# A two-layer hybrid attention block with the order of every engine worked out by the framework's other timing model

## The chip, the cores and the metric

The kernel runs on one core of one Trainium2 chip. The metric is the time of one execution on the device in microseconds (us). Before the change it is 3184.43 us, the median of 3 runs (3184.01 to 3186.54). A core has four compute engines that the profile names PE (TensorE, matrix products), ACT (ScalarE), DVE (VectorE) and POOL (GpSimd), and SP (SyncE), which issues the transfers here; PEld is the loading of TensorE's weights, which overlaps its products. Each engine works through its own list of instructions in order.

## The reference, cut to what matters

Two layers over 256 context and 1024 latent tokens of width 1024, in fp32. In each layer one wide projection feeds four branches, each of width 256; their outputs are projected, gated, summed and projected out.

```
p = (layer_norm(x) * (1 + scale) + shift) @ w_in           # and the same for the context tokens
A: neighbourhood attention, 4 heads of 64 (window 8x16 with a bias, plus all context)
B: latent attention, 4 heads of 96 (64 + 32 rotary)         softmax(q k^T * scale) v, keys: context + latent
C: bidirectional RG-LRU (conv of width 4, one linear scan per direction)
D: grouped-query attention, 4 query heads of 64 over 2 key heads
acc = sum_i sigmoid(m_i) * ((y_i * silu(z_i)) @ w_branch_i)
x   = layer_norm(alpha * x + gate * (acc @ w_out)) * ln_g + ln_b
```

## The kernel before

Every fp32 product is made of three: each operand is split into a high and a low part, and high x high, high x low and low x high are summed (`mm_a`, L271 to L273, and `mm_b`, L279 to L281). Normalized, modulated tokens stand in SBUF, transposed, as `xh` and `xl` for a whole layer.

A layer goes through these stages, which the names in the trace begin with: `g_proj` (projections of D), then `m_proj` and `a_proj` (projections of B and A) woven with `lru` (C) and `g_att` (attention of D), then `m_att` (attention of B), `a_att` (attention of A), `merge`, `last` (the fourth branch's merge) and `outp`. The names `start` and `outp` also stand for the DRAM buffers that were made in those stages. A name of the trace carries no number of the layer; by time, what lies before 1745 us is layer 0.

Attention reads its operands from DRAM. For each head of A and B, and each pair of heads of D, `load_k` (L641) fetches the keys, high rows over low rows, as a tile `ks` of 128 x 1280 (640 KB), and `load_v` (L646) the values, `vs`. A head is worked in units of two query tiles. `load_q` (L632, and L634 for the rotary rows of B) fetches the queries of a unit into one of two `q` buffers; the scores (L618, for A's windows L839) go to PSUM, DVE copies them into a score tile `p` (`pa` in A) with their maxima, and the softmax runs in place on ACT (exp at L592) and DVE. `values` transposes the score tile by blocks of 128 keys (L552), ACT and DVE split the result into two parts (L284, L285), and L568 and L569 multiply it by the values. `values` of a unit is put off until the scores of a later one have been emitted (`defer`), so that scores and values of neighbouring units alternate. Meanwhile `tick` doles out steps of `gates()`, products for the merge that serve as filling for TensorE (L279 to L281 in `m_att` and `a_att`).

The tiles `ks`, `vs`, `p`, `pa`, `y`, and A's bias tables `be` and `bm` share one pool of 12 slots:

```
sl = ctx.enter_context(tc.tile_pool(name="sl", bufs=12))
def load_k(d, blk, r0):
    t = slot(F32R, s="ks")
    sp.dma_start(t.bitcast(F32), d[:, blk, r0:r0 + 64, :])
```

A tile takes a slot when one comes free; its first writer waits for the last reader of the tile that held the slot.

The order of the work is not the order of the Python program. The program emits all instructions once; the framework's `TileContext` then simulates them with a model of the time of each, and from this it decides the order on every engine, which slot each tile gets, and so what each waits for. No order is written by hand.

Of the kernel before, what the change touches and what calls it, by code (L numbers as in the profile page):

```python
# [45 lines left out]
def hybrid_kernel(ctx: ExitStack, tc, a):  # L46
    nc = tc.nc
# [26 lines left out]
    def weave(*streams):  # L74
        """run step generators side by side, in proportion to their expected numbers of steps"""
        live = [[0, n, label, gen] for label, gen, n in streams]
        while live:
            s = min(live, key=lambda s: (s[0] + 0.5) / s[1])
            phase[0] = s[2]
            s[0] += 1  # L80
            if next(s[3], live) is live:
                live.remove(s)
# [3 lines left out]
    def tick(w=1.0):  # L86
        """emit the share of the filling steps that goes with w units of work"""
        fill["due"] += w * fill["rate"]
        while fill["due"] >= 1.0:
            fill["due"] -= 1.0  # L90
            if next(fill["gen"], fill) is fill:
                fill["rate"] = fill["due"] = 0.0
# [20 lines left out]
    def spare():  # L113
        """a [128, 512] tile out of all that are free outside of the branches"""
        turns[0] += 1
        tag = ("tmp", "ph", "tmp", "pl", "tmp", "ph", "pl")[turns[0] % 7]
        return tp.tile([128, 512], F32, tag=tag, name=nm("spare"), bufs=3 if tag == "tmp" else 2)
# [33 lines left out]
    def modulation(l, base, ncols, out, stage, sw):  # L151
        """out["m"] [128, 2, n]: column chunks of silu(cond) @ w_mod + b_mod for both conditions"""
        acc = ps_v.tile([128, 512], F32, tag="pv", name=nm("pm"))
        g = 4
        w_ = ncols // g
        n = ncols // 128
        bm = lc.tile([128, 16], F32, tag="bm", name=nm("bm"))
        sp.dma_start(bm[:, :n], a["b_mod"][l, :, base // 128:base // 128 + n])
        for k in range(KC):
            for h in range(ncols // sw):  # L160
                w = stage()
                c0 = base + h * sw
                sp.dma_start(w, a["w_mod"][l, k * 128:(k + 1) * 128, c0:c0 + sw])
                for j in range(sw // w_):
                    q = 32 * (h * sw // w_ + j)
                    pe.matmul(acc[q:q + 2, :w_], sc[:, k, :], w[:, j * w_:(j + 1) * w_],
                              start=k == 0, stop=k == KC - 1)
                yield
        tps = tbank()
        for j in range(g):  # L170
            row = tmp()
            act.copy(row[0:2, :w_], acc[32 * j:32 * j + 2, :w_])
            for i in range(w_ // 128):
                c = j * (w_ // 128) + i
                pe.transpose(tps[:, 2 * c:2 * c + 2], row[0:2, i * 128:(i + 1) * 128], ident[0:2, 0:2])
        mc = lc.tile([128, 2, 16], F32, tag="modc", name=nm("modc"), bufs=4)
        dve.tensor_tensor(mc[:, :, :n].rearrange("p s n -> p n s"),
                          tps[:, :2 * n].rearrange("p (n s) -> p n s", s=2),
                          bm[:, :n, None].to_broadcast([128, n, 2]), ALU.add)
        if n == 16:  # L180
            dve.tensor_scalar(mc[:, :, 8:16], mc[:, :, 8:16], 1.0, None, ALU.add)
        out["m"] = mc
        yield
# [82 lines left out]
    def mm_a(ps, xs, ws, n0, n1, first=True, last=True):  # L266
        """ps[tok, n] = sum_k x[:, k]^T w[k][:, n0:n1] with operands in two exact parts."""
        nk = len(ws)
        for k in range(nk):
            (xh, xl), (wh, wl) = xs(k), ws[k]  # L270
            pe.matmul(ps, xh, wh[:, n0:n1], start=first and k == 0, stop=False)  # L271
            pe.matmul(ps, xh, wl[:, n0:n1], start=False, stop=False)
            pe.matmul(ps, xl, wh[:, n0:n1], start=False, stop=last and k == nk - 1)  # L273
# [13 lines left out]
    def layer(l, xh, xl, need_ctx, gate, finish, side, side2, ahead=None):  # L287
# [27 lines left out]
        def put_t(dst, t, first, src, rows=128):  # L315
            """transpose column blocks of src [tok, 128*n] to dst[first+i][:, tile t] in two parts"""
            n = len(src)
# [13 lines left out]
        def put_v(dst, t, src3):  # L331
            """src3 [tok, heads, 64] -> per head (high | low) parts"""
            n = src3.shape[1]
            vt = tp.tile([128, 4, 128], F32R, tag="ph", name=nm("vt"), bufs=2)
            hi_lo(vt[:, :n, :64], vt[:, :n, 64:], src3)
            sp.dma_start(dst[t * 128:(t + 1) * 128], vt.bitcast(F32)[:, :n, :])

        def rope(y, t2, h, e, cs, sn, t):
            """axial rotation of y [tok, h, 4*e] in place; t2 [tok, h*4*e] is scratch"""
            w = 4 * e  # L340
# [9 lines left out]
        def project(ws, first_col, n, take=mm):  # L350
            """tokens @ weights tile by tile; the last two together, which frees the weights sooner"""
            for t in range(TT - 2):
# [11 lines left out]

# [1 line left out]
        def g_steps():  # L366
# [43 lines left out]

# [1 line left out]
        def put_u(i, c, y):  # L412
            """branch output times silu of its gate, to DRAM"""
            w = load_chunk(w_in, C_Z + 256 * i + 128 * c)
# [10 lines left out]
        def lru_steps():  # L425
            cols = lc.tile([128, 22], F32, tag="lrucols", name=nm("lrucols"), bufs=1)
            sp.dma_start(cols, a["lru_cols"][l])
            cw, cb, ba, bx, lam = cols[:, 0:8], cols[:, 8:10], cols[:, 10:14], cols[:, 14:18], cols[:, 18:22]
            # -8 * softplus(-lam), softplus by max(-lam, 0) + 2 atanh(e / (2 + e)), e = exp(-|lam|)
            f = [lc.tile([128, 4], F32, tag=f"sp{i}", name=nm("sp"), bufs=1) for i in range(5)]  # L430
# [19 lines left out]
            for c in range(2):  # L450
# [30 lines left out]
                for d in range(2):  # L481
# [16 lines left out]
                    act.activation(r, r, AF.Exp, scale=ca[:, dc])  # L498
                    # 1 - a^2 = t (1 + a^2), t = tanh(-log a)
                    h = slot(s="lruo")  # L500
# [18 lines left out]

# [1 line left out]
        later = []  # L521

        def defer(f, keep):
            """run f after the stages put off before it, all but the newest keep of them now"""
            later.append(f)
# [3 lines left out]
        def attend(h, y, units, loadq, scores, vt):  # L529
            """units: (query tiles, value blocks); rows of y that belong to head h get the output"""  # L530
            o = 64 * (h % 2)
# [52 lines left out]
        def softmax(pt, mx, ns, spans, scale, qi):  # L584
            """rows of pt hold scores / scale with segment maxima mx; spans: column ranges in use"""
            nb = small(1, "nb")
# [40 lines left out]
        def load_q(d, blk, r0, t0, nq, rope=None):  # L627
            """moving side of the scores: the high rows twice, the low rows twice, and the rope rows"""
            t = tp.tile([128, 3, 256], F32R, tag="q", name=nm("q"), bufs=2)
# [8 lines left out]
        def load_k(d, blk, r0):  # L638
            """high rows over low rows"""
            t = slot(F32R, s="ks")  # L640
# [7 lines left out]

# [1 line left out]
        def g_att():  # L650
# [10 lines left out]

# [1 line left out]
        pre = []  # L663

        def m_load():
            """tables and raw weights of the latent branch, ahead of their use"""
            tab = slot(w=896, s="mtab")
# [93 lines left out]

# [1 line left out]
        def m_att():  # L763
# [15 lines left out]

# [1 line left out]
        def a_steps():  # L781
# [15 lines left out]

# [1 line left out]
        def a_att():  # L799
# [72 lines left out]
        def gates():  # L872
            """the merge gates, before their sigmoid, of the branch that is merged last, to DRAM"""
            for c in range(KC):
# [23 lines left out]

# [1 line left out]
        acc = [None] * KC  # L900
# [38 lines left out]

        # the last branch: its gates are there; the sum goes in two parts where xm was  # L940
        phase[0] = f"last{l}"
# [31 lines left out]

# [1 line left out]
        phase[0] = f"outp{l}"  # L975
# [48 lines left out]
    def xm_group(t0, nt):  # L1024
        """xm of nt tiles, one block of channels at a time"""
        s = 1 if t0 < CT else 0
# [64 lines left out]
def _constants(np):  # L1091
    """arrays that depend on the shapes alone"""
    pos = np.arange(SEQ)
# [74 lines left out]
```

## Time and profile before

| | |
|---|---|
| median of the runs | 3184.43 us |
| span of the profiled execution | 3176.4 us |
| TensorE busy | 2806.6 us (88%) |
| loading of TensorE's weights | 2317.9 us (73%) |
| VectorE busy | 1659.0 us (52%) |
| ScalarE busy | 1382.4 us (44%) |
| GpSimd busy | 208.7 us (7%) |
| transfers, mean | 88 GB/s |
| chain that ended last | PE 63%, DMA 17%, DVE 5%, ACT 4%, SP's queue 3% |

The profile gives one execution on the chip. Its own time is that span; the medians of the runs count 8.0 us more, which lie around the span. Busy shares are means over stages of different kinds, so the table says little about any one of them: the merge keeps TensorE nearly always busy, the attention stages do not. In a row of the view of busy time by stretch, further down, stand the start and end, the length, the busy time of PE, PEld, DVE, ACT and POOL with their numbers of instructions, the granted TensorE clock as a share of full speed, the busy share of the 16 DMA engines, and GB/s. The stages of layer 0 in the trace: `g_att` with projections about 300 to 548 us, `m_att` 548 to 832, `a_att` 832 to 1091, `merge` 1091 to 1570; of layer 1, in the same order: 1994 to 2213, 2213 to 2476, 2476 to 2708, and 2708 to 3035.

### The profile page before, as it was taken

What the parts mean: (1) busy time and instruction counts of PE and PEld (TensorE: products, weight loads), DVE (VectorE), ACT (ScalarE), POOL (GpSimd) and SP (SyncE); (2) the same over time, 40 slices, a digit from 0 to 9 for tenths busy, and PEclk for the clock granted to TensorE, in tenths of its full rate; (3) what the DMA queues carried; (4) which work ended last, traced back from release to release, by engine and by line L of the source; (5) the groups of instructions that cost most, each with busy time, mean ns of one, the idle gap of its engine ahead of it and who ended that gap; (6) DMA issues with size and microseconds to landing.
All of it is one profiled execution on the core that took longest, in us unless ns stands there. A gap on an engine that the chain in (4) does not pass through costs nothing.

```text
span 3176.4 us, 40938 instructions
## 1 busy us (share of the span) xinstructions
PE 2806.6 (88%) x14798; PEld 2317.9 (73%) x14798; DVE 1659.0 (52%) x4049; ACT 1382.4 (44%) x2546; POOL 208.7 (7%) x273
## 2 busy tenths in 40 slices
PE   7999978778878999999999899878777688999998
PEld 4787767666767877777768787667666576888877
DVE  5666655555555512232377656556566456223356
ACT  4366655545555512121234456555555455222230
POOL 1200000000000000000042210000000100000031
PEclk9999989888988999999999999999898889999999
DMA  7233222211233322222353323222212222222142
GB/s 264 80 105 117 63 77 80 77 61 64 65 101 95 92 68 65 63 77 62 99 185 101 117 76 116 84 70 74 77 56 72 86 76 90 77 60 60 54 149 84
DMA packets 304563, 281.01 MB, mean 88 GB/s; under 512 B 23400, under 2 KB 249960, under 8 KB 304360
## 3 DMA queue, kind: packets, MB, share of 16 engines
q1 hardware_dynamic: 304360, 278.40, 28.4%
q8 instruction: 116, 1.90, 0.2%
q14 instruction: 87, 0.71, 0.1%
HBM read 207.67 MB, written 70.66 MB: 88 GB/s over the span
## 4 chain that ended last, share of the span: by engine, by line
PE 63%; DMA 17%; DVE 5%; ACT 4%; SPq 3%; issue 2%; POOL 2%; DVEq 0%; POOLq 0%; ACTq 0%
PE merge__mm L279 6%; PE merge__mm L280 6%; PE merge__mm L281 6%; PE m_att__s L618 3%; DMA m_att__q<-start__qkm 2%; PE a_att__mm L279 2%; PE a_att__mm L280 2%; PE a_att__mm L281 2%; DMA m_att__ks<-outp__qkm 2%; SPq L632 2%; PE m_att__t L552 2%; PE a_att__t L552 2%; PE merge__s L279 2%; PE merge__s L280 2%; PE merge__s L281 2%
## 5 line engine op out<-in xcount | busy, mean ns | idle before, releaser
L279 PE MATMUL merge__mm<-xh,merge__whi 128*128 128x512 f32 (+1 forms) x960 | 360.3, 375 | 0.0
L281 PE MATMUL merge__mm<-xh,merge__wlo 128*128 128x512 f32 (+1 forms) x960 | 354.8, 370 | 0.0
L280 PE MATMUL merge__mm<-xl,merge__whi 128*128 128x512 f32 (+1 forms) x960 | 354.8, 370 | 0.0
L279 PEld LDWEIGHTS merge__mm<-xh,merge__whi 128*128 128x128 f32 x960 | 181.5, 189 | 63.1 <-issue 21.6
L618 PE MATMUL m_att__s<-m_att__ks,m_att__q 128*128 128x512 f32 (+1 forms) x400 | 126.7, 387 | 96.9 <-DMA m_att__ks<-outp__qkm 47.4
L233 ACT CAST merge__whi<-merge__wraw 128x512 fp32r<-128x512 f32 x144 | 79.1, 551 | 290.4 <-PE merge__mm L280 243.9
L281 PEld LDWEIGHTS merge__mm<-xh,merge__wlo 128*128 128x128 f32 x960 | 181.6, 189 | 30.7
L280 PEld LDWEIGHTS merge__mm<-xl,merge__whi 128*128 128x128 f32 x960 | 181.7, 189 | 28.9
L928 ACT ACTIVATE merge__tmp<-merge__mm 128x512 f32<-128x512 f32 (+1 forms) x120 | 66.4, 553 | 312.0 <-PE merge__mm L281 311.2
L234 DVE TENSOR_TENSOR merge__wlo<-merge__wraw,merge__whi 128x512 fp32r<-128x512 f32 x144 | 86.4, 601 | 193.3 <-ACT merge__whi L233 187.9
L620 DVE TENSOR_SCALAR_CACHE_REDUCE m_att__p<-m_att__s 128x512 f32<-128x512 f32 (+1 forms) x200 | 113.7, 588 | 115.3 <-PE m_att__s L618 114.3
L284 ACT CAST m_att__ph<-m_att__t 128x512 fp32r<-128x512 f32 x164 | 94.5, 584 | 171.7 <-PE m_att__t L552 126.3
L934 DVE TENSOR_TENSOR merge__tmp<-merge__s,merge__tmp 128x512 f32<-128x512 f32 (+1 forms) x80 | 51.1, 638 | 220.6 <-PE merge__s L281 220.6
L618 PEld LDWEIGHTS m_att__s<-m_att__ks,m_att__q 128*128 128x128 f32 x400 | 76.3, 206 | 112.3 <-DMA m_att__ks<-outp__qkm 42.2
L285 DVE TENSOR_TENSOR g_att__pl<-g_att__t,g_att__ph 128x512 fp32r<-128x512 f32 x154 | 104.7, 688 | 84.8 <-ACT g_att__ph L284 70.9
L618 PE MATMUL g_att__s<-g_att__ks,g_att__q 128*128 128x512 f32 (+1 forms) x400 | 110.0, 381 | 38.6 <-DMA g_att__ks<-outp__qkg 19.6
L285 DVE TENSOR_TENSOR m_att__pl<-m_att__t,m_att__ph 128x512 fp32r<-128x512 f32 x164 | 111.1, 687 | 55.6 <-ACT m_att__ph L284 54.9
L620 DVE TENSOR_SCALAR_CACHE_REDUCE g_att__p<-g_att__s 128x512 f32<-128x512 f32 (+1 forms) x200 | 112.0, 586 | 42.2 <-PE g_att__s L618 41.3
L284 ACT CAST g_att__ph<-g_att__t 128x512 fp32r<-128x512 f32 x154 | 88.1, 583 | 100.6 <-PE g_att__t L552 52.4
L568 PE MATMUL g_att__pv<-g_att__ph,g_att__vs 128*128 128x256 f32 x308 | 98.1, 326 | 30.6 <-ACT g_att__ph L284 29.9
L279 PE MATMUL a_att__mm<-xh,a_att__whi 128*128 128x512 f32 (+1 forms) x304 | 119.0, 391 | 1.6 <-ACT a_att__tmp L885 1.6
L962 POOL TENSOR_TENSOR merge__acc<-merge__acc,last__spare 128x512 f32<-128x512 f32 (+1 forms) x40 | 55.9, 1421 | 939.0 <-DVE last__spare L961 938.8
(425 smaller groups left out, 7870.4 us busy)
## 6 DMA issues: line engine op xcount, KB each, us to landing
merge__wraw<-in_w_in_dram SPq DMA_DIRECT2D x96, 256.0 KB
mod__wm<-in_w_mod_dram SPq DMA_DIRECT2D x48, 256.0 KB
g_proj__wm<-in_w_mod_dram SPq DMA_DIRECT2D x16, 512.0 KB
a_att__wraw<-in_w_in_dram SPq DMA_DIRECT2D x32, 256.0 KB
last__wraw<-in_w_out_dram SPq DMA_DIRECT2D x32, 256.0 KB
merge__wraw<-in_w_branch_dram SPq DMA_DIRECT2D x48, 128.0 KB
g_att__q<-start__qkg SPq DMA_DIRECT2D x40, 128.0 KB
m_att__q<-start__qkm SPq DMA_DIRECT2D x40, 128.0 KB
```

The costliest lines, as they stand in the source:

```text
L233: act.copy(hi[:, :n], raw[:, :n])
L234: dve.tensor_sub(lo[:, :n], raw[:, :n], hi[:, :n])
L279: pe.matmul(ps, wh, xh, start=first and k == 0, stop=False)
L280: pe.matmul(ps, wh, xl, start=False, stop=False)
L281: pe.matmul(ps, wl, xh, start=False, stop=last and k == nk - 1)
L284: act.copy(hi, src)
L285: dve.tensor_sub(lo, src, hi)
L552: pe.transpose(tb[:n, c:c + 128], pts[qi][:, col:col + n], ident)
L568: pe.matmul(pv[:, :nq], vt[:n, vb, :], ph[:n, w], start=first, stop=False)
L618: pe.matmul(s[:, :w], qs[:, j, qi * 128:(qi + 1) * 128], k[:, c0:c0 + w], start=j == 0, stop=j == len(ks) - 1)
L620: dve.tensor_scalar(pt[:, c0:c0 + w], s[:, :w], scale, None, ALU.mult, ALU.max, accum_out=mx[:, ns:ns + 1])
L928: act.activation(sgm[:, :g[1]], pm[:, :g[1]], AF.Sigmoid)
```

## The change

One argument is passed to the framework, and comments and docstrings are blanked, which leaves every line number as it was:

```
-    with tile.TileContext(nc) as tc:
+    with tile.TileContext(nc, schedule_with_timeline_sim=True) as tc:
```

With it the framework simulates the same emitted instructions with another timing model, and takes the order on each engine and the slots of the pools from that. The two programs hold the same 14670 matrix products and the same 1260 transfers of SP; ACT's table loads, which the framework puts in after the order is fixed, go from 77 to 54 (at L420, the sigmoid of the branches' gates, from 27 to 15; at L592, the exp, from 22 to 12; L957 from 2 to none; L433 from 1 to 2). In the merge stages few products move; in the attention stages nearly all do.

The first place is TensorE in `m_att` of layer 1, where the scores of the second head (its K tile is `ks_4740`) have ended and those of the third (`ks_4880`) are about to begin. Before, the rows ahead of the first score of the new head are transpositions of the tiles `p_4812` and `p_4820`, the second last unit of the old head, products with the values, and filling:

```order
L569 MATMUL m_att1__pv_4828_21492<-m_att1__pl_4843_21547,m_att1__vs_4741_21180 128x256
L568 MATMUL m_att1__pv_4828_21492<-m_att1__ph_4842_21546,m_att1__vs_4741_21180 128x256
L569 MATMUL m_att1__pv_4828_21492<-m_att1__pl_4843_21547,m_att1__vs_4741_21180 128x256
L552 MATMUL m_att1__t_4866_21630<-ident_90,m_att1__p_4812_21444 128x128
L552 MATMUL m_att1__t_4866_21630<-ident_90,m_att1__p_4820_21468 128x128
L552 MATMUL m_att1__t_4866_21630<-ident_90,m_att1__p_4812_21444 128x128
L552 MATMUL m_att1__t_4866_21630<-ident_90,m_att1__p_4820_21468 128x128
L279 MATMUL m_att1__mm_4775_21293<-xh_102,m_att1__whi_4623_20698 128x512
L280 MATMUL m_att1__mm_4775_21293<-xl_103,m_att1__whi_4623_20698 128x512
L281 MATMUL m_att1__mm_4775_21293<-xh_102,m_att1__wlo_4624_20699 128x512
L618 MATMUL m_att1__s_4886_21710<-m_att1__ks_4880_21698,m_att1__q_4883_21703 128x512
```

After, what stands ahead of it belongs to the head's first unit (`p_4743`, `p_4751`), without filling:

```order
L568 MATMUL m_att1__pv_4794_21364<-m_att1__ph_4799_21379,m_att1__vs_4741_21180 128x256
L569 MATMUL m_att1__pv_4794_21364<-m_att1__pl_4800_21380,m_att1__vs_4741_21180 128x256
L568 MATMUL m_att1__pv_4794_21364<-m_att1__ph_4799_21379,m_att1__vs_4741_21180 128x256
L569 MATMUL m_att1__pv_4794_21364<-m_att1__pl_4800_21380,m_att1__vs_4741_21180 128x256
L552 MATMUL m_att1__t_4804_21400<-ident_90,m_att1__p_4743_21187 128x128
L552 MATMUL m_att1__t_4804_21400<-ident_90,m_att1__p_4751_21211 128x128
L552 MATMUL m_att1__t_4804_21400<-ident_90,m_att1__p_4743_21187 128x128
L552 MATMUL m_att1__t_4804_21400<-ident_90,m_att1__p_4751_21211 128x128
L568 MATMUL m_att1__pv_4794_21364<-m_att1__ph_4802_21392,m_att1__vs_4741_21180 128x256
L618 MATMUL m_att1__s_4886_21710<-m_att1__ks_4880_21698,m_att1__q_4883_21703 128x512 x2
L618 MATMUL m_att1__s_4886_21710<-m_att1__krs_4582_20569,m_att1__q_4883_21703 128x512
```

Between the last score of the old head and the first of the new one there are now 8 transpositions and 9 products of 256 columns, where there were 8 transpositions, 4 such products and 6 of filling; the transpositions lag the scores by more units than before.

The second place is SP at the same head. `[waits ...]` names the engines and DMA queues on which an entry waits. Before, the K load stands behind the queries of the head's first unit, and the V load right behind it:

```order
L632 DMA m_att1__q_4883_21703<-outp0__qkm_3479_15831 128x1x256 [waits DMAHW2_49,DMAHW1_49,DMAHW7_49,DMAHW0_49,PE_49]
L634 DMA m_att1__q_4883_21703<-outp0__qkm_3479_15831 64x1x256
L632 DMA m_att1__q_4883_21703<-outp0__qkm_3479_15831 128x1x256
L634 DMA m_att1__q_4883_21703<-outp0__qkm_3479_15831 64x1x256
L641 DMA m_att1__ks_4880_21698<-outp0__qkm_3479_15831 128x1x1280 [waits DMAHW3_49,DVE_49]
L646 DMA m_att1__vs_4881_21700<-outp0__vm_3482_15834 128x10x128 [waits DMAHW4_49,Activation_49]
L632 DMA m_att1__q_4934_21915<-outp0__qkm_3479_15831 128x1x256 [waits DMAHW6_49,DMAHW5_49,PE_49]
```

After:

```order
L632 DMA m_att1__q_4883_21703<-outp0__qkm_3479_15831 128x1x256 [waits DMAHW2_49,DMAHW1_49,DMAHW3_49,DMAHW0_49,PE_49]
L634 DMA m_att1__q_4883_21703<-outp0__qkm_3479_15831 64x1x256
L632 DMA m_att1__q_4883_21703<-outp0__qkm_3479_15831 128x1x256
L634 DMA m_att1__q_4883_21703<-outp0__qkm_3479_15831 64x1x256
L641 DMA m_att1__ks_4880_21698<-outp0__qkm_3479_15831 128x1x1280 [waits DMAHW4_49,PE_49]
L632 DMA m_att1__q_4934_21915<-outp0__qkm_3479_15831 128x1x256 [waits DMAHW6_49,DMAHW7_49,DMAHW5_49,PE_49]
L634 DMA m_att1__q_4934_21915<-outp0__qkm_3479_15831 64x1x256
L632 DMA m_att1__q_4934_21915<-outp0__qkm_3479_15831 128x1x256
L634 DMA m_att1__q_4934_21915<-outp0__qkm_3479_15831 64x1x256 [waits DMAHW0_49]
L646 DMA m_att1__vs_4881_21700<-outp0__vm_3482_15834 128x10x128 [waits DMAHW1_49,DVE_49,PE_49]
```

The V load went behind the queries of the second unit, and the K load now waits for PE: its slot is that of `ks_4740`, the K tile of the head before, and is freed by that head's last score. Before, its slot was that of `p_4743`, freed by a transposition well ahead of that.

## Rows read from the trace of the kernel before

**Rows 1.** Busy time by stretch: attention stages of both layers, and layer 0's merge.

```profile
300.00:548.00 248.00, 211.73 (x1332) 185.26 (x1331) 154.93 (x446) 148.19 (x244) 0.00 (x0) 0.93 0.24 75
548.00:832.00 284.00, 215.29 (x1246) 186.73 (x1245) 153.45 (x433) 146.31 (x236) 0.00 (x0) 0.87 0.23 72
832.00:1091.00 259.00, 224.88 (x1321) 195.17 (x1322) 140.69 (x464) 139.75 (x292) 20.28 (x24) 0.91 0.27 84
1091.00:1570.00 479.00, 471.67 (x2317) 364.35 (x2316) 123.78 (x214) 89.56 (x172) 0.00 (x0) 0.99 0.26 71
...
1994.00:2213.00 219.00, 181.76 (x1141) 157.88 (x1141) 137.62 (x387) 126.40 (x198) 0.00 (x0) 0.94 0.23 72
2213.00:2476.00 263.00, 196.88 (x1143) 169.92 (x1143) 144.62 (x391) 136.47 (x207) 0.00 (x0) 0.88 0.23 72
2476.00:2708.50 232.50, 192.76 (x1064) 160.63 (x1065) 121.93 (x413) 125.94 (x256) 20.02 (x24) 0.90 0.27 85
```

**Rows 2.** What PE waited for: total us, times, longest.

```profile
PE m_att__s L618 <- DMA m_att__ks<-outp__qkm: 47.4, 4, 14.4
PE a_att__s L839 <- DMA a_att__q<-outp__qka: 37.2, 6, 14.6
PE m_att__s L618 <- DMA m_att__ks<-start__qkm: 33.3, 3, 12.1
PE g_att__pv L568 <- ACT g_att__ph L284: 29.9, 10, 8.2
PE a_att__s L618 <- DMA a_att__q<-start__qka: 19.7, 4, 10.2
PE g_att__s L618 <- DMA g_att__ks<-outp__qkg: 19.6, 2, 12.0
PE m_att__pv L568 <- ACT m_att__ph L284: 15.5, 3, 6.9
PE m_att__s L618 <- DMA m_att__q<-start__qkm: 14.7, 10, 2.9
...
PE a_att__s L839 <- DMA a_att__ks<-outp__qka: 11.0, 1, 11.0
PE g_att__s L618 <- DMA g_att__ks<-start__qkg: 10.6, 1, 10.6
PE a_att__s L618 <- issue: 9.3, 1, 9.3
```

**Rows 3.** PE in order of time: start, length, what, idle before it and its releaser.

```profile
412.93 1.19 PE L618 MATMUL g_att__s<-g_att__ks,g_att__q 128*128 128x256 f32 x4 [10.57 <-DMA g_att__ks<-start__qkg]
...
680.14 0.28 PE L569 MATMUL m_att__pv<-m_att__pl,m_att__vs 128*128 128x256 f32 x1
680.26 0.60 PE L552 MATMUL m_att__t<-ident,m_att__p 128*128 128x128 f32 x4
680.62 0.36 PE L568 MATMUL m_att__pv<-m_att__ph,m_att__vs 128*128 128x256 f32 x1
...
686.48 0.28 PE L281 MATMUL m_att__mm<-xh,m_att__wlo 128*128 128x256 f32 x1
697.51 0.77 PE L618 MATMUL m_att__s<-m_att__ks,m_att__q 128*128 128x256 f32 x2 [10.75 <-DMA m_att__ks<-start__qkm]
...
2583.39 0.77 PE L839 MATMUL a_att__s<-a_att__ks,a_att__q 128*128 128x512 f32 x1 [4.66 <-DMA a_att__q<-outp__qka]
```

**Rows 4.** SP's DMA issues around one new head, in order of time.

```profile
677.50 1.43 SPq L641 DMA_DIRECT2D m_att__ks<-start__qkm  x1
678.97 2.79 SPq L646 DMA_DIRECT2D m_att__vs<-start__vm  x1
684.17 10.31 SPq L632 DMA_DIRECT2D m_att__q<-start__qkm  x1
```

**Rows 5.** Busy time while only that head's K load was left.

```profile
686.00:696.00 10.00, 0.76 (x5) 0.49 (x3) 0.91 (x2) 3.67 (x6) 0.00 (x0) 0.79 0.13 52
```

**Rows 6.** ACT's table loads at the sigmoid: busy, mean ns.

```profile
L420 ACT ACT_TABLE_LOAD x27 | 34.6, 1283 | 5.7 <-DVE lru__lruo L422 5.2
```

## The prediction

> **What bounds the kernel now.** The profiled span is 3176.4 us; the median of the runs, 3184.43, is 8.0 above it. The view of busy time by stretch comes first. In the merge TensorE is busy 471.7 of 479 us at a granted clock of 0.99: nothing is to be had there but fewer products, and the order of a merge hardly moves. In the six attention stretches the difference of length and busy time is 36.3, 68.7, 34.1, 37.2, 66.1 and 39.7 us, together 282, and the granted clock is 0.87 to 0.94 [rows 1]. The change must win or lose there. No other engine is the bound: VectorE, the next, is busy 121 to 155 us in each of them.
>
> The view of what TensorE waited for says on what. Eight of the rows are first scores of a new head (L618, L839) that wait for its K tile or its queries: 47.4 + 37.2 + 33.3 + 19.7 + 19.6 + 11.0 + 10.6 + 9.3 = 188 us. Two more are products with the values that wait for the split of the transposed scores (L568 behind L284): 29.9 + 15.5 = 45.4. Queries inside a head cost little: 14.7 us in 10 waits, the longest 2.9 [rows 2].
>
> The timeline shows how a head's start stalls. In the third head of layer 0's latent attention SP issues the K load at 677.50, the V load at 678.97, and the next unit's queries at 684.17 [rows 4]; TensorE has work until 686.48 + 0.28 and then stands 10.75 us, till the K tile is there at 697.51 [rows 3]. So 20.0 us go by from issue to use, of which 9 are covered. From 686 to 696 little but this load is in flight, and it moves 52 GB/s on 0.13 of the 16 engines, that is on 2 of them [rows 5]. At that rate its 640 KB need 12.6 us. A head therefore starts without a stall only if 12.6 to 20 us of TensorE's work lie between the moment when the K load can go out and its first use.
>
> **The change part by part.**
>
> *K loads of ten heads.* The order shown at the third head of layer 1's latent attention is the pattern: the K load now needs the slot that the K tile of the head before leaves with its last score. From there to the first use stand 8 transpositions, 9 products of 256 columns and a half-filled score. In the trace a product of 256 columns goes by in 0.12 us and four transpositions in 0.36 (680.14 to 680.26, 680.26 to 680.62) [rows 3]; so 2 x 0.36 + 10 x 0.12 = 1.9 us of work remain to cover the load. I counted all twenty heads in this way. In ten the slot is now freed late, with these covers: second head of D 8.0 us in layer 0 and 1.1 in layer 1; first head of B 3.3 and 4.5; third of B 2.4 and 1.9; first of A 2.4 and 1.9; third of A 5.7 and 1.7. They sum to 32.9 us; by the same count the ten slots were free 12 to 32 us ahead of the use. In the trace these ten heads stalled 77.5 us: eight stalls from 10.57 (at 412.93) to 4.66 (at 2583.39), and two heads without one [rows 3].
>
> A K load takes 12.6 us by its rate or 20.0 by the whole way from issue to use. The way shown had a V load of the same size right behind it, which the new order sends later, so I go between them, nearer to the lower: 16. Then the ten heads stall 10 x 16 - 32.9 = 127 us (93 to 167), which is **+50 us** (+16 to +90).
>
> *Other head starts.* In layer 1's attention A the queries of a head went out behind K, V and both bias loads; now they go right behind K. Two stalls of that kind, at the second and fourth heads, lie in the row of 37.2 us [rows 2]; they can lose as much as V and bias held them up: **-15** (-26 to 0). The first head of D in layer 0 loses cover, 13 us to 6 to 10: **+8** (0 to +10).
>
> *Second units.* In layer 0 the second unit of a head now comes 0.7 to 3.5 us of TensorE's work after the first (2.5 to 14 before), and its queries stand right behind the K load on SP. Such an entry took 10.31 us to go out behind K and V [rows 4]. For eight such heads I take 2 us each, about what query waits cost now [rows 2]: **+15** (0 to +50, where 6 of the 10.31 show each time). Elsewhere the time from a free query buffer to its use falls from some 12.5 us of work to 8: **+5** (0 to +15).
>
> *Transpositions and values.* The new order puts more TensorE work between a transposition and its product with the values, 2.6 to 4.5 us at the median against 1.7, so waits behind the split should shrink. But the longest of them, 8.2 and 6.9 us [rows 2], are not of that kind: they are ACT standing behind something late, which 3 us don't cover. And the steps of filling, which lay between, now come in blocks. I take **-15** of the 45.4 (-45 to +30).
>
> *Table loads.* 23 fewer, at 1283 ns [rows 6], are 29.5 us of ACT. ACT is busy about 126 to 148 us of stretches of 219 to 284 [rows 1], so most of it lies beside other work: **-5** (-29.5 to 0). The Trainium skill (ScalarE: Activation LUTs, What ACT_TABLE_LOAD costs) adds a drain of some 1380 ns to each switch; the row shows the 1283, and none shows the drain. By the page 23 loads would give ACT 61 us back; were all of it on the path, the sum would be 43 + 5 - 61 = -13, an estimate that speaks against a slower kernel and falls into the first rival below.
>
> *Merge, projections, output:* nearly the same order, **0** (-5 to +5).
>
> Sum: 50 - 15 + 8 + 15 + 5 - 15 - 5 = +43 us. Span 3176.4 + 43 = 3219; with the 8.0 around it **3227 us**, 1.3% slower.
>
> **The rivals.**
>
> *It gets faster by what the new order does better.* A head's slot was free early before, and yet most heads stalled: the load's way, not the slot, may be what counts. If K loads without V and bias behind them land in the 12.6 us of their rate, the ten heads cost +16 at most. Then the queries of A give back 26, values 45, and table loads some 10; second units cost 10. That is 16 - 26 - 45 - 10 + 10 = -55: about 3130. For it speaks that the waits of L568 start at ACT [rows 2], which has 23 loads less; against it, that 1 to 8 us of cover are less than the 12.6 us of the rate alone, so that no row lets a head start without a stall.
>
> *Nothing much moves.* Stalls change places: the ten heads +16 to +30, the queries and values -30. Time 3180 to 3190. For it: before, too, eight of the ten stalled, and a stall can grow only by the cover lost. Against it: this asks several terms of different causes to cancel.
>
> *Much slower.* The queries are late as well. Each second unit then waits behind the K load on the same queue (+50), the ten heads stand the full 20 us (+90), and filling in blocks leaves the values' waits as they are (0). With the falling clock behind longer stalls (0.87 where they are thickest, 0.99 without them [rows 1]) that is 140 - 15 + 8 + 5 - 5 = +133: about 3317. For it: a query entry took 10.31 us to go out behind K and V. Against it: V goes later now.
>
> *The argument does nothing that TensorE feels:* excluded by the order, in which nearly all attention products move.
>
> **How the numbers follow.** Forecast +43, its own range +10 to +90: 45%. Much slower, beyond +90: 18%. Little moves, -10 to +10: 13%, half of it inside what counts as no change (0.2%, 6.4 us, about what a measurement of this kernel can tell). Faster beyond -10: 24%. So faster 0.27, the same 0.08, slower 0.65. The range leaves out about a tenth on either side: 3135 to 3300.
>
> **What would show it.** Right: in the profile after, first scores of a new head wait for `ks` in at least seven of the ten heads, 11 to 18 us each, and the sum of the head rows goes from 188 to 220 or more; the second and fourth head of A in layer 1 stall less; SP issues the K load within 2 us of the old head's last score. Wrong: if the K tiles land within 13 us of their issue and the head rows sum to less than 190; if waits of L568 fall by more than 30 us or grow beyond 70; or if the merge stretches, which I hold at zero, move by more than 10 us.

## The result, and the profile after

The changed kernel takes 3450.36 us (median of 4 runs, 3447.23 to 3453.35), the kernel before 3185.48 beside it: a ratio of 1.082, 95% interval 1.0801 to 1.0838. It is 265 us slower. The forecast was slower by 1.3%, 3227 us, with 3300 as the upper end; the direction was right and the size far off.

The spans of the two profiled executions, on which all readings below rest, lie 275 us apart and not 265. In every run with both figures a time is only 1.7 to 2.2 us above its span, so most of the 8.0 us that the prediction adds to the span before is that this execution was a faster one than the median.

The page of the profile after: its span, TensorE's busy time, and TensorE's granted clock in 40 slices in tenths.

```profile
span 3451.5 us, 41058 instructions
...
PE 2877.8 (83%) x14798; PEld 2384.5 (69%) x14798; DVE 1669.8 (48%) x4049; ACT 1352.0 (39%) x2523; POOL 206.4 (6%) x273
...
PEclk9998988978799899999999999879978879999999
```

The span grew by 275.1 us. TensorE is busy 71.2 us longer with the same products, and so idle 203.9 us longer. The view of busy time by stretch says where; its columns are those of [rows 1], the stretches are those between the first scores of successive attention stages, layer 0's merge (1253 to 1721), and layer 1's projections up to its first attention score (1902 to 2180).

```profile
337.00:592.00 255.00, 202.72 (x1164) 175.62 (x1164) 152.75 (x454) 130.93 (x216) 0.00 (x0) 0.89 0.22 69
592.00:933.00 341.00, 248.39 (x1394) 214.52 (x1395) 161.59 (x448) 146.69 (x242) 0.00 (x0) 0.84 0.20 64
933.00:1253.00 320.00, 247.38 (x1369) 211.35 (x1369) 141.97 (x470) 140.16 (x298) 19.54 (x24) 0.87 0.23 71
1253.00:1721.00 468.00, 465.60 (x2304) 362.34 (x2304) 123.04 (x212) 89.03 (x173) 0.00 (x0) 1.00 0.27 71
...
1902.00:2180.00 278.00, 236.28 (x1173) 201.63 (x1171) 158.71 (x334) 136.50 (x307) 34.83 (x58) 0.92 0.31 95
2180.00:2421.00 241.00, 173.11 (x1012) 148.39 (x1012) 132.02 (x374) 116.58 (x181) 0.00 (x0) 0.87 0.20 64
2421.00:2712.00 291.00, 212.82 (x1234) 184.53 (x1234) 148.94 (x400) 136.48 (x211) 0.00 (x0) 0.87 0.21 66
2712.00:2987.00 275.00, 205.35 (x1103) 172.20 (x1103) 127.01 (x421) 123.94 (x259) 19.55 (x24) 0.86 0.24 73
```

All six attention stretches lost: 255 us against 248, 341 against 284 and 320 against 259 in layer 0, 241 against 219, 291 against 263 and 275 against 232.5 in layer 1. Their granted clock was 0.87 to 0.94 before [rows 1] and is 0.84 to 0.89. The merge did not lose: its stretch is 468 us at 1.00, where it was 479 at 0.99, and TensorE is busy 6 us less in it, with 13 products fewer. Ahead of the attention both layers lost. Layer 0 reaches its first attention score at 337 us and not at 301, and layer 1 reaches its own 278 us after its projections begin, where it took 249 at a granted clock of 0.96:

```profile
1745.00:1994.00 249.00, 225.75 (x1153) 190.02 (x1151) 158.76 (x334) 137.87 (x302) 38.11 (x56) 0.96 0.34 104
```

What TensorE waited for, the view of [rows 2] after the change (total us, times, longest):

```profile
PE m_att__s L618 <- issue: 47.3, 3, 18.3
PE a_att__s L839 <- DMA a_att__q<-start__qka: 46.4, 14, 12.1
PE a_att__s L839 <- DMA a_att__q<-outp__qka: 37.9, 10, 12.5
PE m_att__s L618 <- DMA m_att__ks<-start__qkm: 36.1, 3, 12.9
PE m_att__s L618 <- DMA m_att__ks<-outp__qkm: 34.7, 2, 22.4
PE g_att__s L618 <- DMA g_att__ks<-outp__qkg: 32.7, 2, 18.4
...
PE m_att__s L618 <- DMA m_att__q<-start__qkm: 26.7, 17, 3.5
...
PE g_att__pv L569 <- DVE g_att__pl L285: 17.6, 30, 4.6
PE g_att__s L618 <- DMA g_att__q<-start__qkg: 15.1, 11, 2.5
...
PE g_att__pv L568 <- ACT g_att__ph L284: 11.2, 12, 2.1
PE a_att__mm L279 <- ACT a_att__tmp L885: 11.0, 10, 2.0
```

Two such rows before, which [rows 2] leave out:

```profile
PE g_att__pv L569 <- DVE g_att__pl L285: 4.3, 5, 2.5
...
PE a_att__s L839 <- DMA a_att__q<-start__qka: 3.0, 2, 2.3
```

Most of the large rows are still first scores of a head; the three waits of the first row, for which the profile shows no releaser (issue), are such too. New are the many small ones: at L839 A's queries in layer 1 make TensorE wait 10 times instead of 6 [rows 2], in layer 0 14 times instead of 2, and `g_att__pv L569` waits 30 times for DVE's low part of the transposed scores, where it waited 5 times. The longest wait of L568 in D's attention, 8.2 us before [rows 2], is 2.1.

Two sums over all of TensorE's records put this in order. By the length of the idle piece, before and after: 0.3 to 3 us, 93 pieces with 99 us and 210 with 228; 3 to 6 us, 39 and 44 us; over 6 us, 21 pieces in both, 214 and 281 us. So 129 of the 204 us are short waits, and 67 are long ones. By what the product behind it was: first scores of a head 178 to 249 us, first scores of a unit with new queries 0 to 44, other scores 45 to 82, products with the values 63 to 53, transpositions and filling 2 to 30, everything outside of the attention 71 to 107. (The 9 us that are left in either profile lie at the ends of the span. The prediction's 188 us for first scores are 10 more than the 178, because the rows for A's queries hold waits inside heads too.)

The busy time follows from the clock: TensorE ran at 1.2 GHz, the lower of its two levels, for 344 us before and for 597 after, and 191 and 323 us of its busy time fall in there. Products of 256 columns follow each other 0.21 us apart at that level (2552.95 to 2553.16 in the trace after) and 0.12 at the full one [rows 3]. If about half of the busy time at the lower level is loss, it is 95 and 162 us: 66 more, an estimate, and nearly all of the 71.

### The profile page after: what moved, and what is told of

Read it like the earlier page. It is cut to its first block, busy times and chain, and to the rows that moved or that the text cites. A ratio compares the mean times of both kernels' runs of the same rounds, so it can differ in the third digit from the quotient of the medians.

```text
span 3451.5 us, 41058 instructions
## 1 busy us (share of the span) xinstructions
PE 2877.8 (83%) x14798; PEld 2384.5 (69%) x14798; DVE 1669.8 (48%) x4049; ACT 1352.0 (39%) x2523; POOL 206.4 (6%) x273
## 4 chain that ended last, share of the span: by engine, by line
PE 60%; DMA 19%; DVE 7%; ACT 7%; issue 4%; SPq 3%; POOL 0%; POOLq 0%; DVEq 0%; ACTq 0%
PE merge__mm L279 6%; PE merge__mm L280 6%; PE merge__mm L281 6%; DMA a_att__q<-start__qka 3%; PE m_att__s L618 2%; DMA m_att__q<-start__qkm 2%; PE a_att__mm L279 2%; PE a_att__mm L280 2%; PE a_att__mm L281 2%; PE merge__s L280 1%; PE merge__s L281 1%; PE merge__s L279 1%; PE m_att__t L552 1%; PE g_att__s L618 1%; PE a_proj__mm L271 1%
## 5 line engine op out<-in xcount | busy, mean ns | idle before, releaser
L285 DVE TENSOR_TENSOR m_att__pl<-m_att__t,m_att__ph 128x512 fp32r<-128x512 f32 x164 | 111.5, 687 | 72.2 <-ACT m_att__ph L284 71.2
L618 PEld LDWEIGHTS g_att__s<-g_att__ks,g_att__q 128*128 128x128 f32 x400 | 73.3, 208 | 105.6 <-issue 42.2
L839 PE MATMUL a_att__s<-a_att__ks,a_att__q 128*128 128x320 f32 (+1 forms) x128 | 49.1, 448 | 115.3 <-DMA a_att__q<-start__qka 46.4
L285 DVE TENSOR_TENSOR a_att__pl<-a_att__t,a_att__ph 128x512 fp32r<-128x512 f32 (+2 forms) x142 | 87.8, 626 | 100.3 <-ACT a_att__ph L284 99.6
```

Source lines behind the costliest of these rows:

```text
L285: dve.tensor_sub(lo, src, hi)
L618: pe.matmul(s[:, :w], qs[:, j, qi * 128:(qi + 1) * 128], k[:, c0:c0 + w], start=j == 0, stop=j == len(ks) - 1)
L839: pe.matmul(sa[:, :n0], qsl[i], kd[:, k0:k0 + n0], start=i == 0, stop=i == 1)
```

## Experiments

**Loads over more DMA engines.** K loads lead with a dimension of two, and so do the query loads. The first pair of runs splits the K load, the second the query loads too (shown for the rows of all three branches; the rotary rows alike).

```
-            sp.dma_start(t.bitcast(F32), d[:, blk, r0:r0 + 64, :])
+            for i in range(2):
+                sp.dma_start(t.bitcast(F32)[64 * i:64 * i + 64, :], d[i, blk, r0:r0 + 64, :])
...
-                sp.dma_start(tf[:, i, :nq], d[i, blk, r0:r0 + 64, t0:t0 + nq][None].to_broadcast([2, 64, nq]))
+                for r in range(2):
+                    sp.dma_start(tf[64 * r:64 * r + 64, i, :nq], d[i, blk, r0:r0 + 64, t0:t0 + nq])
```

> The kernel before, with each K load issued as two loads of 64 partitions (high rows, low rows), so that its slowest dimension has 64 elements instead of 2. Theory A (the head starts wait for the K load's own 12.6 us on 2 DMA engines): issue to use falls from about 20 us to 6 to 10, the 178 us of stalls at first scores fall to 30 to 70, and the time to 3010 to 3090. Rival B (the K load is late for other reasons, its queue or its issue): stalls stay above 130 and the time within 40 us of 3185.

> The changed kernel with the same split of the K loads. Theory A (most of the 265 us come from K loads with less cover and from queries queued behind them): head stalls fall from 249 us to 60 to 110, waits of second units from 44 to under 15, and the time to 3150 to 3250, so that its distance to the split kernel before is 100 to 170 us instead of 265. Rival C (what the order does in the projections, the filling and the queries, with the lower clock behind it, is most of the loss): the distance stays above 200 us.

> The kernel before with K loads and query loads split in two each, so that both use more than 2 DMA engines; SP issues twice as many query loads. Theory A: query waits inside heads (45 us) fall to under 25 and the time is 10 to 40 us under that with the K loads alone. Rival D (SP's issue time is what counts for queries): not faster than with the K loads alone, or slower.

> The changed kernel with K and query loads split. Theory A: score waits within heads fall from 82 us to under 45, second-unit waits vanish, and the distance to the kernel before with the same split is 60 to 130 us, made of projections, filling and clock. Rival C: the distance stays above 200 us.

Measured against the kernel before (3188.96): with K split 3015.56 under the first model (0.9454, 0.9435 to 0.9473) and 3272.88 under the other (1.0253, 1.0222 to 1.0285); with K and queries split 2814.69 (0.8826, 0.8808 to 0.8844) and 3028.27 (0.9503, 0.9472 to 0.9533). Theory A was right about the load, and too low: under the first model the first scores of the heads wait 17 us in all with K split, where it expected 30 to 70, and none of them with both split. The query loads gave 201 us more, where it expected 10 to 40; waits at the other scores of the heads went from 56 to 1 us with them, and those at the products with the values from 60 to 5. Theory A was wrong about the change: the two orders stay 257 and 214 us apart, as rival C said. With K split, the head stalls of the changed kernel came down to 74 us as expected (60 to 110), but first scores with new queries still wait 30 us and not under 15. D was wrong: SP's extra issues cost nothing that shows.

What TensorE waited for with both loads split, first model (the three largest rows):

```profile
PE g_proj__pm L166 <- DMA g_proj__wm<-in_w_mod_dram: 12.0, 13, 8.9
PE g_proj__t L321 <- DVE g_proj__tmp L348: 8.1, 8, 2.2
PE merge__s L279 <- ACT merge__uh L284: 7.6, 2, 7.4
```

And under the other model:

```profile
PE g_att__pv L569 <- DVE g_att__pl L285: 14.0, 31, 1.9
PE g_proj__pm L166 <- DMA g_proj__wm<-in_w_mod_dram: 13.4, 10, 9.6
PE a_att__mm L279 <- ACT a_att__tmp L887: 13.3, 14, 2.0
PE m_att__pv L569 <- DVE m_att__pl L285: 10.1, 20, 1.3
PE m_proj__t L321 <- DVE m_proj__tl L285: 9.3, 6, 3.0
PE m_proj__mm L271 <- DVE m_proj__tmp L715: 9.0, 3, 4.0
```

Nothing of the attention is among the first; in the second it is ACT and DVE in the attention and the projections that are waited for. Layer 0's latent attention, first model and other model, by stretch:

```profile
500.00:696.00 196.00, 195.56 (x1256) 171.96 (x1255) 151.52 (x433) 147.42 (x236) 0.00 (x0) 1.00 0.40 103
```

```profile
524.00:775.00 251.00, 222.81 (x1394) 195.32 (x1395) 160.48 (x449) 146.54 (x243) 0.00 (x0) 0.98 0.33 87
```

TensorE is idle 0.4 us against 28.2. (The second stretch holds 1394 products against 1256; the new order puts products of A's projections and of D's attention there, and the filling is nearly the same, 312 against 301.) Over the whole span, pieces of 0.3 to 3 us sum to 51 us in 59 pieces and 174 in 189: +122, much as in the pair without the split, though those over 6 us are as good as gone (16 us and 10). By the product behind them, the 212 us between these two spans are: scores of all kinds 1 to 40 us, products with the values 5 to 50, transpositions and filling 2 to 32, everything outside of the attention 70 to 110, and 59 us of longer busy time.

**Where in the program.** Only a part of each layer is put into a block that is ordered by itself, with the first model as control and with the other; outside, the first model orders both.

```
+        with tc.block(name=f"bt{l}", schedule_with_timeline_sim=True):
...
             run(f"m_att{l}", m_att())
...
             run(f"a_att{l}", a_att())
```

> Control: the kernel before with the stages m_att and a_att of each layer put into a block of their own that is ordered by itself, still with the first timing model. The boundary costs something, since nothing is moved across it and the K load at the block's start has no cover: 3200 to 3300 by every theory.

> The same blocks, ordered by the other timing model; everything outside them by the first. Theory A (the loss arises in the latent and neighbourhood attention, where the trace has +170 of the +204 us of idle time with D's attention): +120 to +190 us over the control. Rival C (half of the loss or more comes with the projections, the recurrence and D's attention ahead): under +100.

> Control: the kernel before with the projections, the recurrence and D's attention of each layer in a block of their own, ordered by the first timing model: 3200 to 3300 by every theory.

> The same blocks ordered by the other timing model. Theory A: +50 to +110 us over the control, from about +37 of idle time in projections and recurrence, +37 in D's attention, and the clock. Rival C: over +130. If the two stretches' differences sum to 200 to 300, they are independent of each other and the merge has no part.

B's and A's attention: 3305.19 and 3420.91, +116 us. Projections, recurrence and D's attention: 3260.97 and 3381.06, +120. They sum to 236 of 265, so both parts lose, and 29 us are left for the merge and for what the blocks' borders change. The sizes don't carry over: the controls alone are 112 and 68 us slower than the kernel before, and in the main pair the same two parts lost 188 and 95 us by the stretches. Both measurements lie between the theories: the attention's part is just under what A expected and above C's 100, the projections' just over A's 110 and under C's 130. In the attention block the control, too, has K loads with little cover, and there the other model's head stalls are smaller, 200 us against 226; it loses by short waits, 128 to 194 us, and by 44 us of longer busy time. So late K loads don't explain that part at all. In the projections' block the waits over 3 us grew more, 284 to 331 us, than the short ones, 139 to 170; 23 us of it are first scores of heads, nearly all in D's attention.

**Slots of their own for K.** Two slots hold nothing but K tiles (in the merge, the high parts), so that a K load waits for no score tile; the rest has 10.

```
-    sl = ctx.enter_context(tc.tile_pool(name="sl", bufs=12))
+    sl = ctx.enter_context(tc.tile_pool(name="sl", bufs=10))
...
+        if s in ("ks", "uh"):
+            return sl.tile([128, w], dt, tag="ks", name=nm(s), bufs=2)
```

> The kernel before with two slots of their own for the K tiles (and the merge's high parts, which use them later) and 10 instead of 12 for the rest, so that a K load waits for no score tile and goes out 24 us of TensorE's work or more ahead of its first use; the load itself is unchanged. By every theory the stalls at first scores (178 us) go to under 20, and the time to 2960 to 3050.

> The changed kernel with the same slots. Theory A (the K tile's slot is what the new order loses by): the 249 us of head stalls vanish and the distance to the kernel before with the same slots falls to under 150 us. Theory C (the bulk is many short waits of TensorE for queries, ACT and DVE all over the attention and the projections, and the lower clock behind them): head stalls vanish here as well, but the distance stays at 180 to 260 us, with waits over 0.3 us still about 100 more.

> The kernel before with the split K and query loads and the slots of their own for K. The head stalls were gone with the split alone, so 2790 to 2840 by every theory, no more than 1% from 2815.

> The changed kernel with both. Nothing waits for K any more, and query waits are short. Theory A: within 100 us of the kernel before with both. Theory C: 150 to 210 us above it, two thirds as idle time in pieces under 3 us at the values, the filling and the projections, one third as slower products at the lower clock.

3138.14 and 3417.44; with the split loads 2840.23 and 3011.89. In neither of the first two has the view of TensorE's waits a row for a K tile any more: the wait that theory A named is removed, and the distance is 279 us, no smaller. C expected it to stay and is right, though above its range. The pair is weaker than it looks, since the K loads themselves are still on few engines: in the changed kernel first scores with new queries now wait 116 us against 22 in the control, and other scores 142 against 77, so much of the wait went from K to the queries. My expectation for the first of them failed by 88 us: the head stalls went, and others came, perhaps because ten slots for score tiles are fewer, which no run shows by itself. Its waits:

```profile
PE g_att__pv L570 <- ACT g_att__ph L286: 49.1, 10, 15.3
PE m_att__s L620 <- DMA m_att__q<-outp__qkm: 31.0, 12, 7.0
PE m_att__s L620 <- DMA m_att__q<-start__qkm: 29.5, 14, 4.6
PE m_att__mm L281 <- DVE a_proj__vt L287: 28.2, 2, 16.5
```

The lines here are two higher than in the kernel before. With both edits 172 us of distance are left, in C's range, but made of other shares than expected: short waits go from 68 to 135 us, which is not two thirds, waits over 3 us from 19 to 69, and TensorE is busy 44 us longer.

**Without filling.** `rate = 0.0` in place of the formula: all gate products run later, ahead of the last merge (loads split).

> The kernel before with split K and query loads (2815 us), and with no steps of filling in the attention: all gate products of the fourth branch run later, ahead of the last merge. Theory E (the first order covers ACT's and DVE's splits because it puts products of filling between a transposition and its use): without them short waits come up as in the new order, and the time grows by 60 to 130 us. Rival F (its scores and projections cover enough): under +40 us.

> The changed kernel with the same two edits (3028 us with filling). Theory E: filling in blocks covers little here, so without it the time grows by less than 40 us and the distance between the two orders falls from 214 to 60 to 140 us. Rival F: the distance stays at 180 us or more, so that the waits have to do with where the other instructions stand.

2871.95 and 3067.37: +57 and +39 to the runs with filling, and 195 us apart. The first lies between the two theories, nearer to E (from 60, where F said under 40): under the first model the filling does cover something, and short waits go from 51 to 78 us without it, far from the 174 of the new order. On the distance F is right (180 or more, where E said 60 to 140). The filling's place is worth some 20 us of the 214, not the bulk.

**Whose order.** Every instruction of the named engines is kept in the order in which the program writes it, under both models (loads split):

```
+    class Pinned:
...
+        def __getattr__(self, name):
+            f = getattr(self.eng, name)
+            return lambda *v, **k: tc.keep_in_program_order(f(*v, **k))
+    pe = Pinned(pe)                     # in the second pair: act and dve
```

> Split K and query loads, first timing model, and every TensorE instruction kept in the order in which the program writes it; the model orders the other engines alone. Against 2815 us without the pin: written order alternates scores and values as coarse blocks, so 2850 to 3100 by every theory. It is the control of the next run.

> The same with the other timing model: TensorE's order is now the same in both, word for word; ACT, DVE, SP and the slots differ. Theory G (where TensorE's own instructions stand makes the short waits): the distance between the two models falls from 214 to under 60 us. Rival H (ACT's, DVE's or SP's order makes them): it stays above 120 us.

> Split K and query loads, first timing model, with ACT's and DVE's instructions kept in the written order; TensorE and SP are ordered by the model. Control of the next run: 2830 to 3100 by every theory.

> The same with the other timing model: ACT, DVE and POOL have the same order in both, TensorE and SP do not. Theory G: the distance stays above 100 us. Rival H: it falls under 60 us.

With TensorE's order the same word for word, 3468.59 and 3380.18: the other model is 88 us faster. With ACT's and DVE's order the same, 4161.50 and 4303.12: it is 142 us slower. The expected times missed, since the written order is far worse than either model's. Both pairs speak for G and against H: what the new model does to ACT, DVE and SP is no loss of its own here, and the loss goes with TensorE's order. It is support and no proof. The pinned kernels are 350 to 1350 us slower than those without pins, so that their distances don't carry over in size; the 88 us are more than the 60 that G allowed, the other way round; in the second pair SP's order differs as well as TensorE's; and a pinned TensorE leaves the other engines less to differ in: of ACT's 2183 instructions 671 stand at another place under the other model, against 1642 without pins.

## Why the prediction was wrong in size

Its steps, with what the trace after has for each.

*What bounds the kernel:* right. TensorE stayed the engine to look at, and the merge lost nothing.

*K loads of ten heads, forecast 127 us of stalls:* the trace has 136.4. The pattern shown in the order came out as read. SP's issues at the third head of layer 1's latent attention, and TensorE at the same place:

```profile
2556.88 0.48 SPq L641 DMA_DIRECT2D m_att__ks<-outp__qkm  x1
2557.54 0.48 SPq L632 DMA_DIRECT2D m_att__q<-outp__qkm  x1
2558.07 9.96 SPq L634 DMA_DIRECT2D m_att__q<-outp__qkm  x1
```

```profile
2559.64 0.38 PE L568 MATMUL m_att__pv<-m_att__ph,m_att__vs 128*128 128x256 f32 x1
2572.29 1.19 PE L618 MATMUL m_att__s<-m_att__ks,m_att__q 128*128 128x512 f32 x2 [12.27 <-DMA m_att__ks<-outp__qkm]
```

The K load goes out at 2556.88, is used at 2572.29, 15.4 us later, and TensorE stands 12.27. In the ten heads issue to use took 15.4 to 21.1 us, 17.5 in the mean, where I took 16. The term was +59 against +50.

*Other head starts, forecast -7:* +12. The second and fourth heads of A in layer 1 hardly gained (14.6 and 11.7 us before, 10.2 and 12.5 after), and the first head of D in layer 0 lost 18 us and not 8. Second and fourth heads of B and the first of D in layer 1, for which I had no term, lost 14; the second and fourth of A in layer 0 gained 16.

*Second units, forecast +15:* +28. In layer 0 all scores of second units waited 7 us before and 35 after, inside the range of 0 to 50.

*Queries elsewhere, forecast +5:* +51. This is the step of the sum that failed most. Nearly all of it lies at the last unit that uses a K tile, just before the next head begins: 8 us before, 59 after. The largest part is two stalls of 12.11 and 10.53 us. In layer 0's attention A two K loads went out so early that no first score waited for them, but they went out ahead of the queries of the unit before:

```profile
989.62 0.51 SPq L641 DMA_DIRECT2D a_att__ks<-start__qka  x1
...
993.37 10.81 SPq L632 DMA_DIRECT2D a_att__q<-start__qka  x2
```

```profile
998.62 0.28 PE L281 MATMUL a_att__mm<-xh,a_att__wlo 128*128 128x256 f32 x1
1011.00 0.60 PE L839 MATMUL a_att__s<-a_att__ks,a_att__q 128*128 128x320 f32 x1 [12.11 <-DMA a_att__q<-start__qka]
```

The K load at 989.62 is followed by query loads whose two issues take 10.81 us together, and the last unit of the old head stalls 12.11. The stall was not removed, it moved one unit ahead. [rows 4] had shown such an entry at 10.31 us; I thought of it behind the K load at second units alone, and there at 2 us. The rest are waits of up to 2.7 us, each too short to be seen in a list of stalls.

*Transpositions and values, forecast -15:* -4; the long waits behind ACT went, as hoped, and short ones for DVE came. *Table loads, -5:* ACT's busy time fell by 30.4 us (1382.4 to 1352.0), about 23 x 1.283 = 29.5, and TensorE gained nothing that shows. The Trainium skill (ScalarE: Activation LUTs, What ACT_TABLE_LOAD costs) would have made it 61 us with its drain; ACT's rows don't show one: at the median ACT stands idle 18 ns before a table load and 12 ns after it.

*Filling, and all stages outside the attention, forecast 0:* +22 and +36. That the merge's order costs nothing was right; that the projections' doesn't was not looked at closely enough. Waits at products of A's and B's projections and of the recurrence went from 18 to 59 us, and the block run puts that stretch, with D's attention, at +120.

*The clock, no term in the sum:* +66, by the estimate above. I named it in a rival and added nothing for it there either.

Sum of what was measured: 59 + 12 + 28 + 51 - 4 + 22 + 36 + 66 = 270 of 275. The step that failed is the assumption under four terms, queries elsewhere, filling, the stages outside the attention and the clock, that what is not a long stall today is covered: they stood at +5 in the sum and measured 175 us. Their waits were priced by their old size, though the order of nearly every attention product had changed, and the lower clock behind the waits was priced at nothing. The mechanism that carried my forecast is real, but it is 59 of 275 us, and the experiments that remove it leave 172 to 279 us of distance.

Of the signs that I had named, some failed too. All ten heads waited for their K tile, but only six of them 11 to 18 us, where I asked for seven; the ten stalls are 7.2 to 22.4. The second head of A in layer 1 stalled less, the fourth did not. The waits of L568 fell by 28 us, just short of the 30 that would have spoken against me, and layer 0's merge stretch moved by 11 us, just beyond the 10. Of the rivals, "much slower" was nearest, for two of its reasons (queries, clock), and its 3317 was still 133 us short.

Not settled is which feature of TensorE's order makes the short waits. The filling's place, K's slot and the loads' length are shown not to be the bulk of it. That products stand in bursts (8 products with the values one after another, from 2557.16 to 2558.88 in the trace after) fits the rows for DVE at L569, but no run took that alone away.

## What to carry to other kernels

When a change reorders nearly every instruction, the list of today's long waits is not the list of what it can cost: every place where a wait is hidden by a microsecond of other work is at stake, and here 117 more short waits cost twice the long ones. Give the clock a term: over the twenty profiles of this case each us that TensorE stood idle went with 0.6 to 1.2 us at 1.2 GHz (361 and 344 before, 565 and 597 after, 79 and 49 with both loads split under the first model), and by the estimate above with 0.2 to 0.4 us of longer products. And look at the loads first: splitting the K and query loads gave 12% under the old order, 374 us, more than the 265 that the new order lost.

## What the runs showed of the hardware

A K load of 640 KB whose slowest dimension is 2 moved 52 GB/s on 0.13 of the DMA engines [rows 5], which is 2 of 16. The Trainium skill (DMA: Bandwidth & Descriptors, Rules for kernel authors) says that a slowest dimension of c < 16 confines a transfer to at most c engines; the trace agrees. With 64 rows in that place (32 for the rotary rows), in the K loads and the query loads, the waits at first scores went from 178 us to none and the kernel from 3188.96 to 2814.69 us, the fastest of all the runs here. At the granted clock the same shows: 0.991 of full speed over that run, 0.913 over the changed kernel.

Such loads also held up what SP issued behind them, [rows 4] and the issue at 993.37 above. The kernel before has 17 DMA entries on SP that take over 8 us, 13.9 the longest, and the changed one 15; 13 of the 17 are query loads or their rotary rows, the rest A's bias tables. Under the same model with the K loads split no entry takes over 6.5 us, with the query loads split too none over 2.5. SP's entries then take 726 us in all where they took 1043, although there are 308 more of them.
